# Two features of x are turned ahead of the first input projection, the other fourteen between the first projections, and the conditioning buffers are open from the start

## The chip, the cores and the metric

The kernel runs on one core of a Trainium2 chip. The metric is the device time of one execution in microseconds (us); lower is better. The engines are named as the profile names them: PE (matrix products and transposes; PEld is its weight load), DVE (vector), ACT (scalar, activations), POOL and SP. Nearly all loads are issued by SP.

## The reference

One step of a hybrid decoder: 256 prompt tokens and 8 x 8 sample tokens (320 in all), model width 2048. What matters here is its beginning:

```python
mod = silu(c) @ w_ada + b_ada                  # 9 conditioning rows, 6 * 2048 columns
sh1, sc1, gt1, sh2, sc2, gt2 = split(mod, 6)
h = rms_norm(x, g_pre_mix) * (1.0 + sc1) + sh1 # 320 tokens x 2048
proj = h @ w_in                                # qa, fa, ia, ga, qd, kvd, kpe_raw, gate_a, gate_b
...
# then: hgrn2 scan and latent attention over a paged cache, two output
# projections, gates, w_o, a second conditioned norm, and the 8192-wide MLP
```

## The kernel before

Every product is built in a way that keeps single precision: a weight tile is split into a rounded part `whi` (a cast on ACT, line 151) and a rest `wlo` (a subtraction on DVE, line 148); the activations are split likewise into `hh` and `hl`; three products are summed (lines 173 to 176). The activations lie feature-major: a "feature" here is a block of 128 of the 2048 columns, for all 320 tokens, so that there are sixteen.

**The start.** x is loaded token-major into three tiles `xt` (line 282). ACT and DVE take the mean square of each token and scale the tile (lines 442 to 448). Then the loop of lines 449 to 459 turns x into the feature-major tile `hraw`: for each of the sixteen features three transposes on PE (one for each `xt` tile) into a bank of the pool `aux` (four banks), and one copy from the bank into `hraw`, on DVE for even features (line 457) and on ACT for odd ones (line 455).

**Conditioning steps.** `ada_gen` (lines 318 to 333) computes `mod` a step at a time: one load of 1,024 KB of `w_ada` and 8 or 16 small products (`aux<-raw,cT` in the profile, x16 records for a step of the early form). The first eight steps make the scales and shifts of features 0 to 3, two steps for each of four pairs of features: steps 1 and 2 scale features 0 and 1, steps 3 and 4 shift them, steps 5 to 8 do the same for features 2 and 3. When a result is complete, it is turned by two transposes (`aux<-ident,adarow`) and added into `mod` (lines 306 to 316). Step 1 stands ahead of the loop over features; steps 2, 3 and 4 stand in it, after features 4, 10 and 15. Their loads go to the pool `wraw` (three buffers), which the weights of the projections use as well.

**First projections.** Behind the loop, `modulate(0, 2)` (lines 461 to 470) applies scale and shift to features 0 and 1 and splits them into `hh` and `hl`. Then come five chunks of features (line 532). In the first chunk (features 0 and 1) six calls of `partial` (lines 393 to 417) follow each other; each loads 512 KB of `w_in`, splits it and runs 24 products into four banks of the pool `acc`. Behind each of the first four of them stands one conditioning step (5 to 8), behind the second also `partial_kpe` (a 64 KB load and 6 products), and ahead of the sixth `modulate(2, 2)`. Steps 5 and later load into the pool `sraw` (three buffers), which line 531 opens only when the pool of the `xt` tiles has been closed: it takes their memory.

**Who sets the order.** The kernel is written as one stream. When it is built, a planner deals the instructions to the engines, each of which then runs its own queue strictly in that order; the planner keeps to the written order except where it reckons that an engine would stand idle and something further down could run. SP's queue of loads is such a queue too: a load whose buffer is not free holds those behind it.

**Memory.** Pools lie on two stacks, left and right; one that is opened where a closed one lay waits for the last readers there. `qst`, `lr` (`qn`, `kr`), `hraw` and the `xt` tiles lie on the left, in this order.

Of the kernel before, what the change touches and what calls it, by code (L numbers as in the profile page):

```python
# [7 lines left out]
F32 = mybir.dt.float32  # L8
# [3 lines left out]
AF = mybir.ActivationFunctionType  # L12
ALU = mybir.AluOpType
# [4 lines left out]
D = 2048  # L18
NP = 256
NB = 8  # L20
NT = 8
NS = NB * NT
N = NP + NS
P = 128
KF = D // P
# [56 lines left out]
def tile_hgrn2_mla_step(  # L82
# [9 lines left out]
    nc = tc.nc  # L92
# [10 lines left out]
    wraw = ctx.enter_context(tc.tile_pool(name="wraw", bufs=3))  # L103
# [37 lines left out]
    def mul(out, a, b, eng=None):  # L141
        (eng or nc.vector).tensor_tensor(out=out, in0=a, in1=b, op=ALU.mult)  # L142
# [75 lines left out]
    def rstd_of(x, tmp, r):  # L218

        nc.scalar.activation(out=tmp, in_=x, func=AF.Ln)  # L220
        last_exp[0] = nc.scalar.activation(out=r, in_=tmp, func=AF.Exp, scale=-0.5)
        mul(tmp, r, r)
        mul(tmp, tmp, x)
        nc.vector.tensor_scalar(out=tmp, in0=tmp, scalar1=-0.5, scalar2=1.5, op0=ALU.mult, op1=ALU.add)
        mul(r, r, tmp)

    def mean_eps(out, ps, n):
        nc.vector.tensor_scalar(out=out, in0=ps, scalar1=1.0 / n, scalar2=EPS, op0=ALU.mult, op1=ALU.add)
# [9 lines left out]
    def pool(name, bufs=1, side="left"):  # L238
        return tc.tile_pool(name=name, bufs=bufs, side=side, reuse_waits="tile")
# [13 lines left out]
    xsm = x_sample.rearrange("b t d -> (b t) d")  # L253
    TOK = ((0, 0, P), (1, P, P), (2, NP, NS))

    qst_stack = ExitStack()
    mq = qst_stack.enter_context(pool("mq"))
    qst = mq.tile([P, 6, NB, NS], F32, name="qst")
    lrstack = ExitStack()
    lr = lrstack.enter_context(pool("lr"))  # L260
    kvd = ckvT
    qn = lr.tile([P, RF, N], F32, name="qn")
    qd = qn
# [2 lines left out]
    xstack = ExitStack()  # L266
    xp = xstack.enter_context(pool("xp"))
    hraw = xp.tile([P, KF, N], F32, name="hraw")
    xqstack = ExitStack()
    xq = xqstack.enter_context(pool("xq"))  # L270
    xt = [xq.tile([P, D], F32, name=f"xt{i}") for i in range(3)]
# [27 lines left out]

    GA, GB = 5184, 7232  # L300
    SH1, SC1, GT1, SH2, SC2, GT2 = 0, 16, 32, 48, 64, 80
    araw = [wraw]

    turned = []

# [12 lines left out]
    def ada_gen():  # L318

        for b0, nb in [(SC1, 2), (SH1, 2), (SC1 + 2, 2), (SH1 + 2, 2)] + \  # L320
                [(m + f, 4) for f in (4, 8, 12) for m in (SC1, SH1)] + [(b0, 4) for b0 in range(GT1, 96, 4)]:
            ps = bank()
            nk = 16 // nb
            for r0 in range(0, KF, nk):
                raw, rv = load_w(w_ada, r0, nk, b0 * P, nb * P, araw[0])
                for k in range(nk):
                    mm(ps[32 * (k % 4):32 * (k % 4 + 1), 0:nb * P], cT[:, r0 + k], rv[:, k], r0 + k < 4, r0 + k >= KF - 4)
                if r0 == KF - nk:
                    row = adap.tile([P, 512], F32, name="adarow")
                    nc.scalar.copy(out=row[:, 0:nb * P], in_=ps[:, 0:nb * P])  # L330
                    turned.append((b0, nb, row))
                yield
                ada_turn()

    ada_steps = ada_gen()
# [57 lines left out]
    def partial(f0, nf, cols, outs):  # L393

        raw = wraw.tile([P, 2048], F32, name="raw")
        rv = raw[:, 0:nf * 512].rearrange("p (k c) -> p k c", c=512)
        rows = w_in[f0 * P:(f0 + nf) * P]
        if cols[1] == cols[0] + 256:
            nc.sync.dma_start(out=rv, in_=rows[:, cols[0]:cols[0] + 512].rearrange("(k p) c -> p k c", p=P))
        else:  # L400
            for i, c0 in enumerate(cols):
                nc.sync.dma_start(out=rv[:, :, 256 * i:256 * (i + 1)],
                                  in_=rows[:, c0:c0 + 256].rearrange("(k p) c -> p k c", p=P))
        ps = [bank(acc) for _ in range(4)]
        for k0 in range(0, nf, 2):
            hv, lv = split_w(rv, k0, 2, 512)
            for k in range(2):
                kk = f0 + k0 + k
                for m in range(4):
                    ms = slice(m * P, (m + 1) * P)  # L410
                    mm3(ps[m][:, 0:N], hv[:, k, ms], lv[:, k, ms], hh[:, kk], hl[:, kk],
                        k0 + k == 0, k0 + k == nf - 1)
        for m in range(4):
            if f0 == 0:
                nc.scalar.copy(out=outs[m], in_=ps[m][:, 0:N])
            else:
                add(outs[m], outs[m], ps[m][:, 0:N])
# [15 lines left out]
        else:  # L433
            add(kr, kr, ps[:, 0:N])

    with xqstack:
        junk = hraw.rearrange("p f n -> p (f n)")
        ssq = xq.tile([P, 3], F32, name="ssq")
        rr = xq.tile([P, 3], F32, name="rr")
        tt = xq.tile([P, 3], F32, name="tt")  # L440
        nc.vector.memset(ssq, 1.0)
        for i, t0, n in TOK:
            ss, rs = ssq[:, i:i + 1], rr[:, i:i + 1]
            nc.scalar.activation(out=junk[0:n, i * D // 2:i * D // 2 + D], in_=xt[i][0:n], func=AF.Square,
                                 accum_out=ss[0:n])
            mean_eps(ss, ss, D)
            rstd_of(ss, tt[:, i:i + 1], rs)
            nc.vector.tensor_scalar(out=xt[i][0:n], in0=xt[i][0:n], scalar1=rs[0:n], scalar2=None, op0=ALU.mult)
        for f in range(KF):
            ps = bank()  # L450
            fs = slice(f * P, (f + 1) * P)
            for i, t0, n in TOK:
                transpose(ps[:, t0:t0 + n], xt[i][0:n, fs], n)
            if f % 2:
                nc.scalar.copy(out=hraw[:, f], in_=ps[:, 0:N])
            else:
                nc.vector.tensor_copy(out=hraw[:, f], in_=ps[:, 0:N])
            if f in (4,10,15):
                next(ada_steps)

    def modulate(f0, nf):
        ada_turn()
# [63 lines left out]
        nc.scalar.dma_start(out=kpe_p[0, 0].rearrange("(i p) c -> p i c", p=P), in_=kt[:, 0:2])  # L526
        nc.scalar.dma_start(out=kpe_s[0].rearrange("b t c -> (b t) c"), in_=kt[0:NS, 2])

    p2stack, sstack, lstack, mstack = ExitStack(), ExitStack(), ExitStack(), ExitStack()
    partb = p2stack.enter_context(pool("p2", 1, "right")).tile([P, 4, 2, N], F32, name="partb")  # L530
    araw[0] = sstack.enter_context(pool("sraw", 3))
    chunks = ((0, 2, 4), (2, 2, 8), (4, 4, 8), (8, 4, 8), (12, 4, 0))
    modulate(0, 2)
    for q, (f0, nf, due) in enumerate(chunks):
        last = q == len(chunks) - 1
        for n, (cols, outs) in enumerate((
                ((4608, 4864), [kvd[:, f] for f in range(4)]),
                ((4096, 4352), [qd[:, f] for f in range(4)]),
                ((0, 1024), [part[:, i, j] for i in (0, 1) for j in range(2)]),
                ((2048, 3072), [part[:, i, j] for i in (2, 3) for j in range(2)]),  # L540
                ((GB, GB + 256), [partb[:, i, j] for i in (0, 1) for j in range(2)]),
                ((GA, GA + 256), [partb[:, i, j] for i in (2, 3) for j in range(2)]))):
            if n == 4 and last:
                araw[0] = wraw
                sstack.close()
                xstack.close()
                lr2 = lstack.enter_context(pool("lr2", 2, "right"))
                mp = mstack.enter_context(pool("mp"))
                lowrank_norms(lr2)
                qh = mp.tile([P, RF, N], F32R, name="qh")  # L550
                ql = mp.tile([P, RF, N], F32R, name="ql")
                split(qh, ql, qn)
                ch = mp.tile([P, RF, NP], F32R, name="ch")
                cl = mp.tile([P, RF, NP], F32R, name="cl")
                split(ch, cl, ckvT[:, :, 0:NP])

            if n == 5 and not last:
                turn_ = modulate(*chunks[q + 1][0:2])
            partial(f0, nf, cols, outs)
            for _ in range((0, (1, 1, 1, 1, 0, 0), (2, 2, 2, 1, 1, 0))[due // 4][n] if due else 0):  # L560
                next(ada_steps)
            if q == 3 and n == 0:
                nc.sync.dma_start(out=cst, in_=consts)
            if n == 1:
                partial_kpe(f0, nf)
                if q == 3:
                    with tc.issue_after(turn_.ins):
                        late_init()
# [6 lines left out]
    lstack.close()  # L575
    p2stack.close()
    init.close()


    nc.gpsimd.memset(qst[64:P, 4], 0.0)  # L580
# [8 lines left out]
    with mstack, pool("mp2", 2) as mp2:  # L589
# [126 lines left out]
        early_proj(0)  # L716
        for m in range(2):
            prompt_values(NH // 2 - 1, m, pend[0][m], pend[1])

    lrstack.close()  # L720


    ostack = ExitStack()
# [559 lines left out]
    with pool("zp") as zp, pool("zp2", 2) as zp2, pool("fraw", 3) as fraw:  # L1283
# [25 lines left out]
        for i, t0, n in TOK:  # L1309
            for j in range(2):  # L1310
# [4 lines left out]
                                     accum_out=ssq2[0:n, i, j:j + 1])  # L1315
# [18 lines left out]
        for q0 in range(0, KF, 2):  # L1334
# [3 lines left out]
            for j in range(2):  # L1338
                f = q0 + j
# [11 lines left out]
    with pool("ml1") as ml1, pool("ml2", 2) as ml2:  # L1351
# [4 lines left out]
        for c in range(NCH):  # L1356
# [19 lines left out]
            for g in range(8):  # L1376
                ps = gemm(w_down, 8 * c, 8, 256 * g, uh, ul)
                bk = out_banks() if last else None
                for m in range(2):
                    f = 2 * g + m  # L1380
# [11 lines left out]
        for q in range(4):  # L1392
            fs = slice(q * 512, (q + 1) * 512)
            for i, t0, n in TOK:
                nc.vector.scalar_tensor_tensor(  # L1395
                    out=zt[i][0:n, fs], in0=zt[i][0:n, fs], scalar=r[0:n, i:i + 1],
# [35 lines left out]
```

## Time and profile before

| | |
|---|---|
| median of 3 runs | 2153.34 us (2153.16 to 2161.1) |
| the profiled execution | 2156.85 us, of which its span is 2154.7 us |
| PE busy | 2105.6 us, 98% of the span |
| DVE / ACT / POOL busy | 1069.3 / 864.2 / 168.7 us |
| moved by DMA | 401.69 MB, mean 186 GB/s |

All times within the trace are counted from the start of the span. PE's busy time is modelled from a pipelined engine, so that a stretch of PE at 100% may still be one in which products follow each other at half the rate; the spacing of the starts tells that.

### The profile page before, as it was taken

The page shows a single profiled execution, that of the slowest core. Times are in us where ns is not written, and L with a number is a line of the kernel's source. Part 1 is how long each engine was busy: PE and PEld are TensorE (multiplying, and loading weights), DVE is VectorE, ACT ScalarE, POOL GpSimd, SP SyncE. Part 2 cuts the span into 40 slices and gives each one's busy share as a digit, 9 for nine tenths or more (in the row PEclk, how much of TensorE's full clock was granted, in tenths as well). Part 3 has the DMA queues.
Part 4 walks back from the last instruction along what each step waited for, and adds up shares of the span by engine and source line. Part 5 has one row for each costly group of instructions (what it writes and reads, how often), then busy time and mean ns, then how long its engine had stood idle before and what let it go on. Part 6 is the DMA issues. An engine that isn't in the chain of part 4 may idle for free.

```text
span 2154.7 us, 34719 instructions
## 1 busy us (share of the span) xinstructions
PE 2105.6 (98%) x14637; PEld 1906.8 (88%) x14637; DVE 1069.3 (50%) x1665; ACT 864.2 (40%) x1312; POOL 168.7 (8%) x167
## 2 busy tenths in 40 slices
PE   6999999999999999999999899999999999999997
PEld 3788989557788889999999599999999999999996
DVE  3555754445765646433544643444444444444455
ACT  4432453333545434333343543434343333333343
POOL 0000001103232211100010000000000000000001
PEclk9999999999999999999999899999999999999998
DMA  8986456444767768766854565445445445445442
GB/s 256 320 301 234 155 190 220 157 126 144 221 226 235 240 211 276 225 210 200 275 184 137 181 189 176 151 145 157 146 149 157 145 149 157 142 151 157 141 152 69
DMA packets 327571, 401.69 MB, mean 186 GB/s; under 512 B 10984, under 2 KB 265528, under 8 KB 324600
## 3 DMA queue, kind: packets, MB, share of 16 engines
q1 hardware_dynamic: 301576, 362.82, 52.3%
q0 software_dynamic: 3584, 21.50, 2.8%
q10 hardware_dynamic: 22256, 15.16, 2.3%
q8 instruction: 115, 1.88, 0.4%
q14 instruction: 40, 0.33, 0.0%
HBM read 387.44 MB, written 12.01 MB: 185 GB/s over the span
## 4 chain that ended last, share of the span: by engine, by line
PE 88%; issue 5%; DVE 3%; DMA 2%; ACT 1%; POOL 1%; SPq 0%; DVEq 0%; ACTq 0%; POOLq 0%
PE acc L136 76%; PE aux L136 8%; PE aux L139 4%; DMA raw<-in_w_in_dram 1%; DVE wlo L148 1%; POOL X L142 1%; ACT whi L151 1%; DMA raw<-in_w_ada_dram 1%; DMA xt<-in_x_prompt_dram 0%; DVE zu L1395 0%; DVE X L148 0%; DVE zg L142 0%; POOL qt L142 0%; ACT X L964 0%; DVE qn L499 0%
## 5 line engine op out<-in xcount | busy, mean ns | idle before, releaser
L148 DVE TENSOR_TENSOR wlo<-raw,whi 128x1024 fp32r<-128x1024 f32 (+1 forms) x493 | 603.8, 1230 | 706.2 <-ACT whi L151 703.5
L151 ACT CAST whi<-raw 128x1024 fp32r<-128x1024 f32 (+1 forms) x493 | 502.9, 1026 | 804.4 <-PE acc L136 665.9
L136 PE MATMUL acc<-hh,whi 128*128 128x320 f32 x1168 | 369.1, 317 | 3.5 <-ACT hh L151 2.3
L136 PE MATMUL acc<-hl,whi 128*128 128x320 f32 x1168 | 361.9, 310 | 0.3 <-DVE hl L148 0.3
L136 PE MATMUL acc<-hh,wlo 128*128 128x320 f32 x1168 | 360.7, 311 | 0.0
L136 PE MATMUL acc<-uh,whi 128*128 128x320 f32 x1024 | 316.7, 309 | 0.0
L136 PE MATMUL acc<-gh,whi 128*128 128x320 f32 x1024 | 316.7, 309 | 0.0
L136 PE MATMUL acc<-gh,wlo 128*128 128x320 f32 x1024 | 316.6, 309 | 0.0
L136 PE MATMUL acc<-gl,whi 128*128 128x320 f32 x1024 | 316.3, 309 | 0.0
L136 PE MATMUL acc<-uh,wlo 128*128 128x320 f32 x1024 | 316.1, 309 | 0.0
L136 PE MATMUL acc<-ul,whi 128*128 128x320 f32 x1024 | 316.1, 309 | 0.0
L136 PEld LDWEIGHTS acc<-hh,whi 128*128 128x128 f32 x1168 | 219.4, 188 | 34.6 <-issue 17.3
L136 PEld LDWEIGHTS acc<-hl,whi 128*128 128x128 f32 x1168 | 219.8, 188 | 2.9 <-DVE hl L148 1.4
L136 PEld LDWEIGHTS acc<-hh,wlo 128*128 128x128 f32 x1168 | 219.0, 188 | 3.0 <-DVE wlo L148 2.5
L136 PEld LDWEIGHTS acc<-gh,whi 128*128 128x128 f32 x1024 | 192.5, 188 | 1.9 <-ACT u L1365 0.8
L136 PEld LDWEIGHTS acc<-uh,whi 128*128 128x128 f32 x1024 | 192.6, 188 | 1.7 <-ACT u L1364 0.8
L136 PEld LDWEIGHTS acc<-gh,wlo 128*128 128x128 f32 x1024 | 192.6, 188 | 0.2
L136 PEld LDWEIGHTS acc<-gl,whi 128*128 128x128 f32 x1024 | 192.6, 188 | 0.0
L136 PEld LDWEIGHTS acc<-ul,whi 128*128 128x128 f32 x1024 | 192.4, 188 | 0.0
L136 PEld LDWEIGHTS acc<-uh,wlo 128*128 128x128 f32 x1024 | 192.4, 188 | 0.0
L136 PE MATMUL aux<-raw,cT 128*32 128x512 f32 (+1 forms) x832 | 115.2, 601 | 16.3 <-DVE tt L142 11.4
L145 POOL TENSOR_TENSOR ssum<-ssum,sqt 128x320 f32<-128x320 f32 x26 | 25.9, 997 | 981.2 <-ACT sqt L1245 980.3
(425 smaller groups left out, 2563.0 us busy)
## 6 DMA issues: line engine op xcount, KB each, us to landing
raw<-in_w_ada_dram SPq DMA_DIRECT2D x96, 1024.0 KB, 6.5
raw<-in_w_up_dram SPq DMA_DIRECT2D x64, 1024.0 KB, 5.7
raw<-in_w_down_dram SPq DMA_DIRECT2D x64, 1024.0 KB, 5.4
raw<-in_w_in_dram SPq DMA_DIRECT2D x60, 1024.0 KB, 5.4
raw<-in_w_o_dram SPq DMA_DIRECT2D x16, 1024.0 KB, 5.7
raw<-in_w_in_dram SPq DMA_DIRECT2D x20, 512.0 KB, 6.0
raw<-in_w_b_out_dram SPq DMA_DIRECT2D x8, 1024.0 KB, 5.8
raw<-in_w_a_out_dram SPq DMA_DIRECT2D x8, 1024.0 KB, 5.4
```

Of the source, the lines that this page charges most:

```text
L136: pe_last[0] = nc.tensor.matmul(out, lhsT=lhsT, rhs=rhs, start=start, stop=stop)
L139: pe_last[0] = nc.tensor.transpose(out=out, in_=in_, identity=ident[:k, :k])
L142: (eng or nc.vector).tensor_tensor(out=out, in0=a, in1=b, op=ALU.mult)
L145: (eng or nc.vector).tensor_tensor(out=out, in0=a, in1=b, op=ALU.add)
L148: return (eng or nc.vector).tensor_tensor(out=out, in0=a, in1=b, op=ALU.subtract)
L151: nc.scalar.copy(out=hi, in_=src)
```

## The change

The three tiles of x are scaled as before. Behind that, and ahead of the first projection, now stand: conditioning step 2, the turning of features 0 and 1 alone, conditioning steps 3 and 4. The other fourteen features are turned behind the first four calls of `partial`: 2, 4, 4 and 4 of them. The pool `sraw` is opened at the outset, below the pool of the `xt` tiles; steps 1, 2 and 4 load into it, step 3 into `wraw`. To make room, `lr` goes to the right stack, `qst` is opened only when `hraw` is closed, and `partb` (the results of the fifth and sixth call) only when the `xt` tiles are closed, ahead of the fifth call. `lr` is closed earlier, behind the five chunks.

```diff
@@
-    qst_stack = ExitStack()
-    mq = qst_stack.enter_context(pool("mq"))
-    qst = mq.tile([P, 6, NB, NS], F32, name="qst")
     lrstack = ExitStack()
-    lr = lrstack.enter_context(pool("lr"))
+    lr = lrstack.enter_context(pool("lr", 1, "right"))
...
     hraw = xp.tile([P, KF, N], F32, name="hraw")
+    sstack = ExitStack()
+    sraw = sstack.enter_context(pool("sraw", 3))
     xqstack = ExitStack()
...
-    araw = [wraw]
+    araw = [sraw]
...
+    def turn_x(f0, nf):
+        for f in range(f0, f0 + nf):
             ps = bank()
...
-            if f in (4,10,15):
-                next(ada_steps)
+
+    next(ada_steps)
+    turn_x(0, 2)
+    araw[0] = wraw
+    next(ada_steps)
+    araw[0] = sraw
+    next(ada_steps)
...
-    p2stack, sstack, lstack, mstack = ExitStack(), ExitStack(), ExitStack(), ExitStack()
-    partb = p2stack.enter_context(pool("p2", 1, "right")).tile([P, 4, 2, N], F32, name="partb")
-    araw[0] = sstack.enter_context(pool("sraw", 3))
+    p2stack, lstack, mstack = ExitStack(), ExitStack(), ExitStack()
+    partb = None
...
+            if q == 0 and n == 4:
+                xqstack.close()
+                partb = p2stack.enter_context(pool("p2", 1, "right")).tile([P, 4, 2, N], F32, name="partb")
...
                 lr2 = lstack.enter_context(pool("lr2", 2, "right"))
+                qst_stack = ExitStack()
+                qst = qst_stack.enter_context(pool("mq")).tile([P, 6, NB, NS], F32, name="qst")
...
             partial(f0, nf, cols, outs)
+            if q == 0 and n < 4:
+                turn_x((2, 4, 8, 12)[n], (2, 4, 4, 4)[n])
...
     init.close()
+    lrstack.close()
...
-    lrstack.close()
```

## Rows read from the trace of the kernel before

**Rows 1.** The page: the share of the chain that ended last by engine.

```profile
PE 88%; issue 5%; DVE 3%; DMA 2%; ACT 1%; POOL 1%; SPq 0%; DVEq 0%; ACTq 0%; POOLq 0%
```

**Rows 2.** Busy time by stretch: the stretch, its length, busy us (and instructions) of PE, PEld, DVE, ACT and POOL, then the granted clock of PE, the busy share of the DMA engines and GB/s.

```profile
17.00:20.00 3.00, 3.00 (x17) 1.52 (x10) 1.05 (x2) 0.46 (x3) 0.00 (x0) 1.00 1.10 347
...
15.60:34.20 18.60, 18.52 (x92) 8.65 (x92) 5.53 (x15) 3.25 (x9) 0.41 (x1) 1.00 0.62 187
...
41.00:44.40 3.40, 3.40 (x12) 2.26 (x12) 1.86 (x2) 0.00 (x0) 0.00 (x0) 0.51 1.11 340
44.40:73.70 29.30, 29.30 (x232) 26.20 (x231) 11.29 (x18) 18.04 (x36) 0.98 (x2) 1.00 0.89 301
73.70:112.00 38.30, 37.85 (x249) 27.13 (x248) 22.12 (x44) 10.81 (x12) 1.42 (x2) 1.00 0.98 343
```

**Rows 3.** The chain that ended last, in order of time, from 15 to 81 us: start, length, engine, tile and line.

```profile
36.48 1.03 PE aux L136 x14
...
38.00 0.45 PE aux L139 x2
...
40.72 1.29 PE acc L136 x4
42.02 0.99 PE aux L136 x2
...
46.76 0.99 PE aux L136 x14
...
73.96 1.04 PE aux L136 x8
...
75.02 6.23 DMA raw<-in_w_ada_dram
```

**Rows 4.** PE's matmuls and transposes in order of time: start, length of the group, tile out<-in, and in brackets the idle time before it.

```profile
15.68 1.94 PE L136 MATMUL aux<-raw,cT 128*32 128x256 f32 x16 [11.38 <-DVE tt L142]
17.55 0.28 PE L139 MATMUL aux<-ident,grow 16*128 16x16 f32 x1
...
17.98 4.58 PE L139 MATMUL aux<-ident,xt 128*128 128x128 f32 x15
22.49 1.93 PE L136 MATMUL aux<-raw,cT 128*32 128x256 f32 x16
24.36 5.55 PE L139 MATMUL aux<-ident,xt 128*128 128x128 f32 x18
...
43.38 0.47 PE L136 MATMUL acc<-hh,wlo 128*128 128x320 f32 x1
43.64 0.47 PE L136 MATMUL acc<-hl,whi 128*128 128x320 f32 x1
...
45.57 0.31 PE L136 MATMUL acc<-hh,wlo 128*128 128x320 f32 x1
45.72 0.31 PE L136 MATMUL acc<-hh,whi 128*128 128x320 f32 x1
```

**Rows 5.** The copies that follow the turning of features 12, 14 and 13 of x (DVE's timeline, then ACT's), for the rate of the transposes.

```profile
34.25 0.49 DVE L457 COPY hraw<-aux 128x320 f32<-128x320 f32 x1 [2.75 <-PE aux L139]
35.40 0.49 DVE L457 COPY hraw<-aux 128x320 f32<-128x320 f32 x1 [0.66 <-PE aux L139]
...
34.83 0.43 ACT L455 COPY hraw<-aux 128x320 f32<-128x320 f32 x1 [1.06 <-PE aux L139]
```

**Rows 6.** SP's queue from the start: issue time, length (with the waits inside a group), line and load.

```profile
4.83 13.20 SPq L161 DMA_DIRECT2D raw<-in_w_ada_dram  x4
24.48 8.33 SPq L399 DMA_DIRECT2D raw<-in_w_in_dram  x2
36.20 0.99 SPq L161 DMA_DIRECT2D raw<-in_w_ada_dram  x2
```

**Rows 7.** Transposes of the paged cache in a stage with the clock at its upper level (PE's timeline).

```profile
378.32 0.38 PE L139 MATMUL aux<-ident,craw 128*128 128x128 f32 x2
378.54 0.38 PE L139 MATMUL aux<-ident,raw 128*128 128x128 f32 x2
```

**Rows 8.** Busy time by stretch of the transposes alone (line 139): stretch, length, PE, PEld, granted clock, DMA share, GB/s.

```profile
376.00:446.00 70.00, 27.71 (x213) 22.58 (x212) 1.00 0.45 154
```

**Rows 9.** Who waited for whom from 38 to 74 us: total, times, longest.

```profile
DVE wlo L148 <- ACT whi L151: 15.7, 7, 5.3
```

**Rows 10.** POOL's timeline: the memsets of `qst`, and the first loads of the paged cache, which take memory of pools closed before.

```profile
0.75 0.52 POOL L580 MEMSET qst<- 64x512 f32 x1 [0.29 <-POOLq L1418]
...
254.10 1.90 POOL L142 TENSOR_TENSOR part<-part,lrsq 128x640 f32<-128x640 f32 x1 [46.08 <-ACT lrsq L473]
...
355.47 0.95 POOL L739 DMA_INDIRECT kraw<-in_cache_kpe_dram,pidx  x1 [0.30 <-issue]
356.73 0.93 POOL L748 DMA_INDIRECT craw<-in_cache_ckv_dram,pidx  x1 [0.30 <-issue]
```

**Rows 11.** PE's timeline where the stage of the paged cache begins.

```profile
365.23 0.84 PE L139 MATMUL aux<-ident,Sp 128*128 128x128 f32 x3
...
371.17 0.64 PE L139 MATMUL aux<-ident,craw 128*128 128x128 f32 x2
```

**Rows 12.** DMA issues of the stretch from 330 to 450 us: load, queue, count, median us from issue to landing.

```profile
craw<-in_cache_ckv_dram,pidx POOLq DMA_INDIRECT x10, 6.8
```

**Rows 13.** The first instructions that touch `qst` after the memsets (the tile's view: min/median/max ns, first and last start in us).

```profile
L664 ACT COPY qst<-qp x8: 239/244/245, 275.9 to 339.6; 64x64 f32<-64x64 f32 x8
```

More of the change, by code (lines that the diff above doesn't have):

```diff
@@ L434, in partial_kpe @@
             add(kr, kr, ps[:, 0:N])
[L436 to L449, printed above, removed]
+    junk = hraw.rearrange("p f n -> p (f n)")
+    ssq = xq.tile([P, 3], F32, name="ssq")
+    rr = xq.tile([P, 3], F32, name="rr")
+    tt = xq.tile([P, 3], F32, name="tt")
+    nc.vector.memset(ssq, 1.0)
+    for i, t0, n in TOK:
+        ss, rs = ssq[:, i:i + 1], rr[:, i:i + 1]
+        nc.scalar.activation(out=junk[0:n, i * D // 2:i * D // 2 + D], in_=xt[i][0:n], func=AF.Square,
+                             accum_out=ss[0:n])
+        mean_eps(ss, ss, D)
+        rstd_of(ss, tt[:, i:i + 1], rs)
+        nc.vector.tensor_scalar(out=xt[i][0:n], in0=xt[i][0:n], scalar1=rs[0:n], scalar2=None, op0=ALU.mult)
+    def turn_x(f0, nf):
+        for f in range(f0, f0 + nf):
             ps = bank()
@@ L540, in tile_hgrn2_mla_step @@
                 ((2048, 3072), [part[:, i, j] for i in (2, 3) for j in range(2)]),
-                ((GB, GB + 256), [partb[:, i, j] for i in (0, 1) for j in range(2)]),
-                ((GA, GA + 256), [partb[:, i, j] for i in (2, 3) for j in range(2)]))):
+                ((GB, GB + 256), (0, 1)), ((GA, GA + 256), (2, 3)))):
+            if q == 0 and n == 4:
+                xqstack.close()
+                partb = p2stack.enter_context(pool("p2", 1, "right")).tile([P, 4, 2, N], F32, name="partb")
+            if n >= 4:
+                outs = [partb[:, i, j] for i in outs for j in range(2)]
             if n == 4 and last:
```

## The prediction

> **What bounds the kernel now.** I read the page first: the chain that ended last lies on PE for 88% of the span [rows 1], so time is gained only where PE waits or runs at a lower rate than it could. Then the table of busy time by stretch, for the part that the change touches. PE is busy in nearly all of 15.6 to 34.2 us, but with slow work; from 44.4 to 73.7 us it is full, and from 73.7 to 112 us it lacks 0.45 us [rows 2]. Then the chain in order of time: step 4 of the conditioning ends at 37.51 us, the first product of the first projection starts at 40.72, and between the two PE does only the 0.45 us of turning the conditioning row [rows 3]. That is a wait of some 2.8 us with nothing to fill it, because every transpose of x stands ahead of it. Last, PE's own order of time, for its rate: six features are turned in 5.55 us from 24.36 on, 0.92 us each [rows 4], while features 12 to 14 follow each other at 0.57 us [rows 5]. The granted clock reads 1.00 in both places [rows 2], but the same shapes run slower in the first, so I go by durations there. [...]
>
> So the front loses time in two ways: fourteen features are turned at the slow rate ahead of the first projection, and PE waits ahead of it.
>
> **Part 1: what stands ahead of the first projection.** Before, step 1 runs at 15.68 us, and PE works without a break to 37.51 [rows 3, 4]. After, the order is step 1, two features, steps 2 to 4. Is the data there? Loads arrive at 347 GB/s [rows 2], so that a step's 1,024 KB take 3.0 us; step 1 had to wait for its load until 15.68 (the idle time in the row is put down to DVE work that does not feed it [rows 4]), so that steps 2, 3 and 4 can start at about 18.7, 21.7 and 24.7 us. A step takes 1.87 us (22.49 to 24.36), the small transposes behind step 1 0.43 us (17.55 to 17.98) [rows 4]. PE: step 1 and these to 17.98, step 2 to 20.6, two features of 0.92 us to 22.4, the first conditioning row (0.6 us at the slow rate, worked out from 0.45 [rows 3]) to 23.0, step 3 to 24.9, step 4 to 26.8. From the end of step 4 to the first product it took 3.21 us (37.51 to 40.72 [rows 3]); I add 0.2 us for the row at the slow rate. The first projection starts at 30.2 us instead of 40.72: 10.5 us earlier.
>
> Its weights must be there too. Their load was issued at 24.48 us, when step 2 had freed the buffer [rows 6]; now steps 1, 2 and 4 use other buffers, and it follows step 4's load directly: 512 KB more, there at about 26.2 us, with the cast and the subtraction inside the 3.4 us that PE waits for the conditioning anyway. Loads of steps 5 and 6 were held until 36.20, when the x tiles were free [rows 6]; now they wait for the products of steps 1 and 2. Nothing on SP is moved behind something later than before. I cost the loads at nothing; were the weights late, each us would count in full.
>
> **Part 2: the first projection.** From its start to the next piece it took 6.04 us (40.72 to 46.76, with 0.99 us of step 5 in a wait for `hl`) [rows 3]. Part of it ran at the lower clock level. After, PE comes to it with less work behind it; how long the lower level lasts there no row shows. Bounds: 24 products at 0.15 us and a wait of 0.9 make 4.5 us; at 0.26 us and with 0.99 they make 7.2 us [rows 3, 4]. I take 6.6, nearer to the slow end, as the stretch ahead of it is slow in the trace of before.
>
> **Part 3: the fourteen features.** 42 transposes on PE, seven copies on DVE and seven on ACT. The copies are cheap: ACT is busy 18.0 and DVE 11.3 of the 29.3 us to 73.7 [rows 2], and seven copies add 3.0 and 3.4 us (0.43 and 0.49 each [rows 5]). On PE they count. Some will fall into the wait of 3.4 - 0.6 = 2.8 us ahead of the first projection, since the planner fills idle time with later work: a memset of `qst`, written behind all five chunks, runs at 0.75 us [rows 10], and step 5 fills the wait for `hl` [rows 3]. Three features of 0.92 us fit. The other eleven cost 0.57 us each, the price of the same transposes at the higher rate [rows 5]: 6.3 us. Bounds: none fits and fourteen cost 8.0 us; five fit and nine cost 3 x 0.11 us each (two transposes of the cache start every 0.22 us [rows 7]), 3.0 us.
>
> **The sum.** Take the point at 73.96 us, where step 9 starts [rows 3]; the work from 46.76 to there, 27.2 us, is the same. After: 30.2 + 6.6 + 27.2 + 6.3 = 70.3, so 3.7 us are gained. The good ends: 30.2 + 4.5 + 27.2 + 3.0 = 64.9, 9.1 us. The bad ends: 30.2 + 7.2 + 27.2 + 8.0 = 72.6, 1.4 us.
>
> **Part 4: the memory moves.** `lr` on the other side, the earlier close of `lr` and the late `partb` cost nothing where their last readers are done: `partb` waits for the last transposes of x, which stand ahead of the fifth call anyway. The two memsets of `qst` (0.52 us each) move from 0.75 us to behind a product on POOL that ends at 256.0 [rows 10]; `qst` is first written at 275.9 [rows 13], so that 19.9 us hide 1.0 us; without that cover it would be 1.0 us. The pools behind `qst` slide down by the size of `lr`, so that the buffers for the paged cache lie on others of the attention's tiles; that is a rival below.
>
> **Behind 73.96 us** I carry the gain through: loads there are issued as buffers come free, which PE's own progress decides, so they move along.
>
> The profiled execution took 2156.85 us, its span 2154.7: 2153.1 us after, with a span of 2151.0. Against the median of 2153.34 us, 3.5 us lower, the forecast is **2149.6 us**, its own range 2144.2 to 2151.9.
>
> **The rivals.**
>
> *Copies that hold PE (the other side).* A moved transpose needs one of four `aux` banks, and a bank comes free only by its copy, which now stands in DVE's and ACT's queues amid the splitting of weights. DVE waited seven times for ACT's cast, 15.7 us in all [rows 9], 2.2 us each; a copy queued behind such a wait holds PE. One such wait in each of the four groups costs 9.0 us: 2153.3 - 3.7 + 9.0 = 2158.6. It outweighs the gain from 0.9 us a group on. For it: the groups of four fill all banks, which conditioning steps share. Against it: both engines are idle much of the time [rows 2], and a copy takes less than its feature. Chance 0.10.
>
> *Turning costs the clock.* In 15.6 to 34.2 us PE, busy all along, with much turning, stayed slow [rows 2, 4]. If each group of transposes between projections brought the lower level for as long as from 41.0 to 44.4 us [rows 2], it would cost 3.4 x 0.49 = 1.7 us, four groups 6.8: 2156.4 us. It decides from the third group on. Against it: from 376 to 446 us transposes are 27.7 of 70 us, and the clock is 1.00 throughout [rows 8]. [...] Chance 0.06.
>
> *The loads take it back.* From 73.7 to 112 us the DMA engines are busy 0.98 of the time, and a piece of 6.23 us on a conditioning load lies on the chain [rows 2, 3]. If that stretch is set by the loads and not by PE, it ends where it did: 2153.3 us. Against it: PE lacks only 0.45 us there [rows 2]. Chance 0.09.
>
> *A later load of the cache.* The first `craw` load is issued at 356.73 us [rows 10]; 6.8 us later it is there [rows 12], for transposes at 371.17 [rows 11]. If the new places make POOL's queue wait until the transposes of `Sp` end at 366.07 [rows 11], it lands at 372.9, 1.7 us late: 2151.3 us. Chance 0.08.
>
> *The order is not what is written.* If the planner puts the transposes ahead of the first projection all the same, PE has the same 21.8 us from 15.68 to 37.51 and then the row's 0.45, without the wait: 37.96 instead of 40.72, a gain of 2.8 us [rows 3, 4], 2150.5. Chance 0.07.
>
> **How the numbers follow.** Forecast 0.60, rivals 0.10, 0.06, 0.09, 0.08, 0.07. The range 2144.0 to 2156.5 us holds all but the first rival and some hundredths of other mishaps. What a measurement of this kernel can tell from no change is about 0.5%, 10.8 us. Even the good ends stop at 9.1 us, so faster by more has 0.03; the dearest rival loses 5.3 us, so slower by more has 0.03; 0.94 lie between.
>
> **What would show it.** In the changed profile the first `acc<-hh,whi` should start near 30 us, steps 2 to 4 near 18.7, 21 to 23 and 25 us, and three or so features be turned ahead of it. From there to the step behind the next chunk PE should show no idle time before transposes (a wait on `hraw` copies is the first rival), and the granted clock should stay at 1.00 once it is up (else the second). The step at 73.96 should come near 70 us, and the same gap should still stand at 112, 260 and 376 us; where it shrinks, the rival of that place was right. I am wrong in the main if the first projection starts early and the point at 73.96 does not move.

## The result: some 4.5 us slower, and the profile after

| | before | after |
|---|---|---|
| median of 20 runs | 2153.8 us (2151.35 to 2161.16) | 2158.92 us (2154.47 to 2165.14) |
| ratio after / before | | 1.0021, interval 1.0011 to 1.003 |
| the profiled execution | 2156.85 us | 2155.09 us, span 2153.3 us |

The changed kernel takes 4.5 us more (0.0021 x 2153.8; interval 2.4 to 6.5). Here and below a ratio and its interval are worked out from all runs of both kernels; it is not the ratio of the two medians, which lie 5.1 us apart here. The change is less than 0.5%, to which I had given 0.94, but it has the other sign than my forecast of 2149.6 us, and the median lies 2.4 us above the upper end of my range, 2156.5. The profiled execution of after happens to be one of its shortest; the last section says why its total must not be used alone.

**The front did what it should.** PE's order of time, in the same columns as [rows 4]:

```profile
15.80 1.93 PE L136 MATMUL aux<-raw,cT 128*32 128x256 f32 x16 [11.50 <-DVE tt L142]
...
18.09 1.33 PE L139 MATMUL aux<-ident,xt 128*128 128x128 f32 x4
19.36 1.94 PE L136 MATMUL aux<-raw,cT 128*32 128x256 f32 x16
...
22.21 1.07 PE L136 MATMUL aux<-raw,cT 128*32 128x256 f32 x16
24.74 1.07 PE L136 MATMUL aux<-raw,cT 128*32 128x256 f32 x16 [1.47 <-DMA raw<-in_w_ada_dram]
26.35 0.44 PE L139 MATMUL aux<-ident,adarow 128*128 128x128 f32 x2 [0.54 <-ACT adarow L329]
26.62 1.16 PE L139 MATMUL aux<-ident,xt 128*128 128x128 f32 x6
29.27 0.85 PE L136 MATMUL acc<-hh,whi 128*128 128x320 f32 x4 [1.49 <-ACT hh L151]
...
46.21 2.30 PE L139 MATMUL aux<-ident,xt 128*128 128x128 f32 x12
```

The four steps stand at 15.80, 19.36, 22.21 and 24.74 us; two features (six transposes at 26.62) fit into the wait ahead of the first projection; this starts at 29.27 instead of 40.72. Four features at 46.21 take 2.23 us to the next instruction at 48.44, 0.56 us each.

**The chain** in order of time, the columns of [rows 3], around the point that answers to 73.96:

```profile
68.54 1.04 PE aux L136 x8
...
69.60 7.59 DMA raw<-in_w_ada_dram
...
77.23 1.07 PE aux L136 x8
```

The point has come 5.4 us forward, from 73.96 to 68.54. Then PE waits 2.13 us for a conditioning load, by its own row:

```profile
77.23 1.07 PE L136 MATMUL aux<-raw,cT 128*32 128x512 f32 x8 [2.13 <-DMA raw<-in_w_ada_dram]
```

From 73.7 to 108.5 us PE is idle for 2.26 us in after and for 0.45 in before, so that 1.9 of the 5.4 us are given back. From 108 to 360 us the same instructions of PE stand 3.56 us earlier than before.

**Then the gain is lost in one place**, where the paged cache begins. POOL's order of time (before: [rows 10], where the same two loads are issued at 355.47 and 356.73 with no wait), then PE's, both of after:

```profile
366.97 0.95 POOL L750 DMA_INDIRECT kraw<-in_cache_kpe_dram,pidx  x1 [15.37 <-PE aux L136]
368.23 0.94 POOL L759 DMA_INDIRECT craw<-in_cache_ckv_dram,pidx  x1 [0.31 <-issue]
```

```profile
365.05 1.65 PE L136 MATMUL aux<-PTp,vv 128*128 128x128 f32 x6
374.08 0.66 PE L139 MATMUL aux<-ident,craw 128*128 128x128 f32 x2 [7.38 <-DMA craw<-in_cache_ckv_dram,pidx]
...
380.60 1.02 PE L136 MATMUL acc<-wlo,qst 128*64 128x512 f32 x4
```

POOL stands 15.37 us at the load of `kraw`, whose buffer is released by a product of PE (`aux` at line 136). The load of `craw` is behind it in the same queue. PE finishes the products `aux<-PTp,vv` and stands idle for 7.38 us. The chain says the same, step by step:

```profile
365.12 1.59 PE aux L136 x6
366.71 0.26 issue
366.97 0.95 POOL kraw L750
367.93 0.31 issue
368.23 5.71 DMA craw<-in_cache_ckv_dram,pidx
373.94 0.14 issue
374.08 5.35 PE aux L139 x24
```

0.26 + 0.95 + 0.31 + 5.71 + 0.14 = 7.37 us: the whole wait. In before the same six products and the `craw` transposes behind them follow each other without a gap:

```profile
369.73 1.65 PE L136 MATMUL aux<-PTp,vv 128*128 128x128 f32 x6
371.17 0.64 PE L139 MATMUL aux<-ident,craw 128*128 128x128 f32 x2
...
376.87 1.03 PE L136 MATMUL acc<-wlo,qst 128*64 128x512 f32 x4
```

So PE is 4.68 us ahead at the `vv` products (365.05 against 369.73), 2.91 us behind at the first `craw` (374.08 against 371.17), and 3.72 us behind from the products of `wlo` on (380.60 against 376.87), a loss of 3.56 + 3.72 = 7.3 us in the stage. The granted clock (the column behind POOL's) in the windows of after, then of before, has a part in what the wait of 7.38 us does not explain:

```profile
364.00:368.00 4.00, 2.70 (x17) 2.38 (x16) 1.02 (x4) 0.00 (x0) 0.95 (x1) 0.50 0.00 0
368.00:372.00 4.00, 0.00 (x0) 0.00 (x0) 0.00 (x0) 0.00 (x0) 2.85 (x4) 0.50 0.81 240
372.00:376.00 4.00, 1.92 (x9) 1.95 (x10) 0.00 (x0) 0.59 (x1) 1.86 (x2) 0.50 1.01 422
376.00:380.00 4.00, 4.00 (x19) 3.33 (x19) 1.91 (x3) 1.17 (x2) 0.00 (x0) 0.50 1.00 422
```

```profile
368.00:372.00 4.00, 4.00 (x27) 3.98 (x27) 1.02 (x4) 0.00 (x0) 0.00 (x0) 0.50 0.68 272
372.00:376.00 4.00, 4.00 (x24) 3.83 (x22) 1.38 (x2) 1.54 (x3) 0.00 (x0) 0.57 0.12 39
376.00:380.00 4.00, 4.00 (x25) 2.08 (x26) 1.99 (x3) 0.80 (x2) 0.37 (x1) 1.00 0.00 0
```

Both kernels fall to the lower level (0.50) here, among products of 8 columns (`128x8`) and small transposes; in after, the wait falls into it and it lasts to 380 us instead of 375.4. From the first `craw` to the products of `wlo` after takes 6.52 us (374.08 to 380.60) and before 5.70 (371.17 to 376.87): the 0.8 us between 2.91 and 3.72. On the other side, after reaches the lower level later in the order of its work: the three transposes of `Sp` ahead of the `vv` products take 0.84 us in before [rows 11] and 0.49 in after, and by the `vv` products the 3.56 us have grown to 4.68. The two nearly cancel, so that the loss of 7.3 us is about the wait itself.

### The profile page after: what moved, and what is told of

It is laid out like the page before. It is cut to its first block, busy times and chain, and to the rows that moved or that the text cites. A ratio compares the mean times of both kernels' runs of the same rounds, so it can differ in the third digit from the quotient of the medians.

```text
span 2153.3 us, 34711 instructions
## 1 busy us (share of the span) xinstructions
PE 2095.7 (97%) x14637; PEld 1902.3 (88%) x14637; DVE 1073.2 (50%) x1665; ACT 863.2 (40%) x1312; POOL 167.2 (8%) x167
## 4 chain that ended last, share of the span: by engine, by line
PE 87%; issue 4%; DVE 3%; DMA 3%; ACT 1%; SPq 1%; POOL 1%; DVEq 0%; ACTq 0%; POOLq 0%
PE acc L136 76%; PE aux L136 8%; PE aux L139 4%; DMA raw<-in_w_ada_dram 1%; DVE wlo L148 1%; DMA raw<-in_w_in_dram 1%; ACT whi L151 1%; SPq L161 0%; DVE zu L1406 0%; DVE X L148 0%; DMA craw<-in_cache_ckv_dram,pidx 0%; POOL qt L142 0%; DVE zg L142 0%; DVE bb L956 0%; POOL X L142 0%
```

## The experiments

**My theory.** `lr` (`qn` and `kr`, 4 x 320 and 320 values, 6,400 bytes of each partition) has left the left stack, so the attention's pools lie 6,400 bytes lower. The first `kraw` buffer now covers a tile `vv` that the last products `aux<-PTp,vv` read, and in POOL's queue the small load, which waited 15.37 us in after, held the large ones behind it. The front itself gains what I forecast.

**The rivals.** Against this theory stand three others: the time is lost because POOL and the load work arrive differently behind an earlier PE, not because of the layout; or the clock alone costs it; and, for the front, that the open conditioning buffers give the gain and not the order of the turning.

### The order of the loads (two kernels)

After, with the `craw` loads of the first two sequences issued ahead of `kraw`:

```diff
             kraw = sc.tile([P, 8, 64], F32, name="kraw")
-            nc.gpsimd.indirect_dma_start(out=kraw.rearrange("p j c -> p (j c)"), out_offset=None, in_=kpe_rows,
-                                         in_offset=off)
+
+            def load_kraw():
+                nc.gpsimd.indirect_dma_start(out=kraw.rearrange("p j c -> p (j c)"), out_offset=None, in_=kpe_rows,
+                                             in_offset=off)
+
+            if b >= 2:
+                load_kraw()
             craws = []
...
+            if b < 2:
+                load_kraw()
             return kraw, craws
```

> The changed kernel, with one difference: for the first two sequences of the paged cache the two large loads (craw) are issued ahead of the small one (kraw); PE's order is the same as in the changed kernel. Theory (queue): the two small loads now lie on memory that the attention's last products (vv) read until 366.6 us, and hold the craw loads behind them in POOL's queue; with craw ahead, its first load is issued near 352 us, PE does not wait 7.4 us at 366.7, and the 3.6 us gained ahead of it are kept: 2150.2 us, 0.998 of before. The small load itself still waits to about 367 us and is needed only some 7 us after the stage's start, so that it costs at most 1 us. Rival (clock): the loss is the longer stretch at the lower clock level (17.1 us in the changed kernel, 10.2 us before); then the order of the loads changes little and the time stays at 2157 to 2159 us.

Measured: 2152.29 us against 2153.56, ratio 0.9985 (0.9971 to 0.9999). POOL, then PE, of this run:

```profile
350.85 0.94 POOL L764 DMA_INDIRECT craw<-in_cache_ckv_dram,pidx  x1 [0.30 <-issue]
367.36 0.95 POOL L752 DMA_INDIRECT kraw<-in_cache_kpe_dram,pidx  x1 [15.57 <-PE aux L136]
```

```profile
365.44 1.65 PE L136 MATMUL aux<-PTp,vv 128*128 128x128 f32 x6
366.88 0.64 PE L139 MATMUL aux<-ident,craw 128*128 128x128 f32 x2
```

`kraw` waits as long as in after, 15.57 us, and it harms nothing: the first `craw` is issued 16.5 us ahead of it and PE has no gap. PE stands 4.62 us ahead of the kernel before at 360 us and again from 376 us on (4.29 in the rows shown, which lie within the lower clock level). The memory conflict is still there; what cost the time was its place at the head of the queue. Between after and this kernel lie 0.0036, 7.8 us (some 4 to 11 us by the two intervals), against the 7.3 us read from the trace.

The same exchange in the kernel before:

> The kernel before with the order of the cache's loads of x1_swap, nothing of the change. Theory (queue): before, neither small load waits, so that putting the large ones ahead gives nothing: the first transposes of the cache stay at 371 us, 2153.6 us, 1.000 of before. Rival: the order of x1_swap is better by itself, whatever the places; then this kernel gains what x1_swap gained over x2_hole, 1 to 2 us. It is a second trace of the front of before as well.

Measured: 2154.09 against 2153.5 us, ratio 0.9997 (0.998 to 1.0013). Where no `kraw` waits, the exchange is worth nothing that shows.

### The layout alone, and the layout put back

Before, with nothing but `lr` moved to the right stack and closed where after closes it; the front is unchanged:

```diff
-    lr = lrstack.enter_context(pool("lr"))
+    lr = lrstack.enter_context(pool("lr", 1, "right"))
...
     init.close()
+    lrstack.close()
...
-    lrstack.close()
```

> The kernel before, with lr on the right stack and closed ahead of the attention, and nothing else of the change; PE's order is that of before. Theory (queue): this alone brings the wait: the first kraw load near 370 us in place of 355.5, PE idle for about 7 us ahead of the first transposes of the cache, 7.3 us slower than before: 2161 us, 1.0034. Rival: the loss comes of the new order of the front, by way of the clock or of the loads of 69 to 113 us; then this kernel takes 2153.8 us as before.

Measured: 2167.63 against 2153.56 us, ratio 1.0054 (1.0034 to 1.0074), from five runs: 11.6 us, more than after itself loses. POOL, then PE:

```profile
371.17 0.95 POOL L738 DMA_INDIRECT kraw<-in_cache_kpe_dram,pidx  x1 [17.01 <-PE aux L136]
```

```profile
369.24 1.65 PE L136 MATMUL aux<-PTp,vv 128*128 128x128 f32 x6
378.40 0.66 PE L139 MATMUL aux<-ident,craw 128*128 128x128 f32 x2 [7.51 <-DMA craw<-in_cache_ckv_dram,pidx]
```

The same wait, 7.51 us, without any change of the front. PE goes from 1.0 us ahead of before to 7.9 us behind, a loss of 8.9 us. So the layout alone does it; after's 4.5 us are net of what the front gains, and here the front gains nothing by the edit. The 1.4 us beyond the wait fall into a longer stretch at the lower clock level, 20.5 us against 10.2 in before (worked out from the granted clock in windows of 4 us; it is 0.50 from 364 to 384 us here). The 8.9 us lie within the interval of the measured loss, 7.3 to 15.9 us; why its middle is higher stays open with five runs.

After, with an unused tile of 6,400 bytes (and a memset of one column of it) that puts the later attention pool back to its old place:

```diff
+    hole = mstack.enter_context(pool("hole")).tile([P, 1600], F32, name="hole")
+    nc.gpsimd.memset(hole[:, 0:1], 0.0)
     with mstack, pool("mp2", 2) as mp2:
```

> The changed kernel, with an unused tile of 6,400 bytes a partition (the size of qn and kr together) between the pools mp and mp2, so that the attention's tiles lie under the buffers of the paged cache as they did before; one memset of a column on POOL is added. Theory (queue): no small load waits, the first craw load is issued near 353 us (before: 356.7, less 3.6), PE does not wait, 2150.2 us, 0.998 of before. Rival (clock): as the changed kernel, 2157 to 2159 us. If x1_swap is fast and this one is not, it is the queue's order but not the place of lr that matters.

Measured: 2153.8 against 2153.56 us, ratio 0.9994 (0.9978 to 1.001). POOL, then PE:

```profile
353.75 0.95 POOL L752 DMA_INDIRECT kraw<-in_cache_kpe_dram,pidx  x1 [0.31 <-issue]
```

```profile
369.44 1.65 PE L136 MATMUL aux<-PTp,vv 128*128 128x128 f32 x6
370.88 0.63 PE L139 MATMUL aux<-ident,craw 128*128 128x128 f32 x2
```

`kraw` is issued at 353.75 and `craw` at 355.01 without a wait, and PE goes from the `vv` products to `craw` without a gap. The wait is gone: PE is 1.71 us ahead of before at 360 us and still 0.94 us ahead from 376 us on. But the front gained only 1.8 us in this trace, because its first projection ran at the lower clock level (0.54 from 28.5 to 36 us, below), and the total, forecast at 0.998, shows no gain.

Two smaller tiles, one run each. With 512 values (2,048 bytes, one `kraw` buffer or one `vv` tile):

> The kernel of x2_hole with the unused tile cut to 2,048 bytes a partition. Worked out from the sizes of the tiles: the buffer of the first small load still lies on the second vv tile, which the last products read. Theory (the place of vv): the first kraw load waits until these products end, and PE is idle for about 7 us ahead of the first transposes of the cache, as in the changed kernel. Rival (any shift loosens it): no wait.

2158.33 us: `kraw` waits 14.96 us, PE 7.43 us for `craw`; 3.82 us ahead become 1.90 behind.

```profile
366.30 0.95 POOL L752 DMA_INDIRECT kraw<-in_cache_kpe_dram,pidx  x1 [14.96 <-PE aux L136]
```

```profile
373.46 0.66 PE L139 MATMUL aux<-ident,craw 128*128 128x128 f32 x2 [7.43 <-DMA craw<-in_cache_ckv_dram,pidx]
```

With 768 values:

> The same with 3,072 bytes: now the first small load's buffer lies on the first vv tile, read for the last time some 20 us earlier, and the second one's on the second vv tile. Theory (the place of vv): the first kraw load and the first craw load go at about 353 us, the second kraw load waits to about 366 us with the craw loads behind it, which are needed only at 380; PE does not wait ahead of the first transposes. Rival (lr's full size is needed): the wait stays about 7 us.

2152.8 us. POOL:

```profile
351.53 0.95 POOL L752 DMA_INDIRECT kraw<-in_cache_kpe_dram,pidx  x1 [0.30 <-issue]
352.79 0.94 POOL L761 DMA_INDIRECT craw<-in_cache_ckv_dram,pidx  x1 [0.30 <-issue]
367.64 0.95 POOL L752 DMA_INDIRECT kraw<-in_cache_kpe_dram,pidx  x1 [13.91 <-PE aux L136]
```

Now the first `kraw` is free and the second waits 13.91 us. Its followers come late, but PE has the first `craw` (transposed at 367.16 without a wait) to work on, and no time is lost: 3.95 us ahead on both sides. 1,024 bytes decide between a loss of 5.7 us and none. Which tile lies under which buffer I take from the releaser in these rows and from the sizes, not from addresses. These two are single runs, and their totals would prove little; the rows of the waits carry the argument.

### The two halves of the front

Both with the tile of 6,400 bytes, so that the cache stage is not in the way. First the early conditioning buffers alone: all sixteen features are turned ahead of the first projection, the steps in their old places.

```diff
+    turn_x(0, 5)
     next(ada_steps)
-    turn_x(0, 2)
+    turn_x(5, 6)
     araw[0] = wraw
     next(ada_steps)
     araw[0] = sraw
+    turn_x(11, 5)
     next(ada_steps)
...
-            if q == 0 and n < 4:
-                turn_x((2, 4, 8, 12)[n], (2, 4, 4, 4)[n])
```

> The kernel of x2_hole with all sixteen features turned ahead of the first projection, steps 2 to 4 behind features 4, 10 and 15 as in the kernel before: the early buffers without the moved turning. Theory (the moved turning gives the gain): the first projection starts near 40 us, the wait ahead of it stays, and the point at which step 9 starts stays within 1 us of 73.96: 2153 us, 1.000 of before. Rival (the early loads give it): that point comes near 69 us and the time is that of x2_hole.

Measured: 2153.78 against 2153.56 us, ratio 0.9995 (0.9981 to 1.001). In the trace the first product stands at 43.55, behind a wait of 2.28 us, and step 9 at 77.69 instead of 73.96; PE stays 3.25 us behind from 100 to 340 us. That is later than either theory said, which had 73 to 75 and 69 us: the front stayed at its slow rate longer (products 0.27 us apart until 48.8 us). In this trace the open buffers alone bring nothing forward.

Then the turning alone: `sraw` is opened only ahead of the fifth call, and steps 1 to 8 load through `wraw`.

```diff
-    sraw = sstack.enter_context(pool("sraw", 3))
...
-    araw = [sraw]
+    araw = [wraw]
...
                 xqstack.close()
+                araw[0] = sstack.enter_context(pool("sraw", 3))
```

> The kernel of x2_hole with the turning moved, but the pool of the conditioning buffers opened only when the x tiles are closed, ahead of the fifth call of the first chunk; until then steps 1 to 8 load into the three buffers of the weights: the moved turning without the early buffers. Theory (both parts are needed): the loads of steps 4 to 8 and of the first projections wait for each other's buffers, PE waits for them in 25 to 70 us, and step 9 starts at 74 us or later: 2154 to 2160 us. Rival (the turning alone gives the gain): step 9 starts near 70 us and the time is that of x2_hole.

Measured: 2152.55 against 2153.5 us, ratio 0.9992 (0.9975 to 1.0009). The first product comes at 30.68 us, so the early start is the order of the turning. Step 9 begins at 67.98, but only two of its products; the other fourteen come at 72.67. At 100 us PE is 0.73 us behind before: the early start is spent. SP shows one cause, the loads of the steps:

```profile
62.16 11.99 SPq L161 DMA_DIRECT2D raw<-in_w_ada_dram  x2
```

Two issues take 11.99 us with the wait for a buffer, and those behind them move too. The forecast time, 2154 to 2160 us, was missed: 2152.55 us is not clear of before either way. So in its one trace neither half alone has PE ahead of before at 100 us. That each half needs the other is not shown by this: neither ratio differs from 1 by more than its interval, and both fronts were longer at the slow rate than after's (with the turning alone the granted clock is 0.57 from 28.5 to 36 us). The share that each half has of the 3.7 us stays open.

## Why the prediction was wrong, point by point

- **What stands ahead of the first projection: right in time, in part by luck.** Steps at 15.80, 19.36, 22.21, 24.74 us (forecast: step 1, then 18.7, 21 to 23, 25). First product 29.27, forecast 30.2. But the sum let PE's own work set these times, with 1.87 us a step. Steps 3 and 4 took 1.07 us each, and step 4 waited 1.47 us for its load, which arrived near the 24.7 us that I had worked out for it.
- **The first projection: its good bound.** It took 4.55 us (29.27 to 33.82, where the next step begins on the chain), forecast 6.6, bound 4.5: in this run the upper clock level was there from the first product on (1.00 from 29.2 to 33.9 us). In the run with the tile of 6,400 bytes it was not (0.54 from 28.5 to 36 us), and there the front gained 1.8 us instead of 3.6.
- **The fourteen features: right.** 0.56 us each (forecast 0.57); two fitted ahead, not three. The rival "turning costs the clock" falls here: the 12 transposes at 46.21 us take 2.23 us, the products behind them (from 49.81 us) start 0.15 us apart, and the granted clock is 1.00 from 44.4 to 68.5 us. Between the projections this trace shows no harm from turning.
- **The point of step 9: 68.54, forecast 70.3** (own bounds 64.9 to 72.6). 5.4 us gained, then 1.9 us given back, most of it in the wait of 2.13 us for a load: the rival "the loads take it back" holds for a part. In the run with exchanged loads, whose front is the same program, no such wait came: 4.8 us ahead at this point, 5.26 at 140 us.
- **The gain of the front: right in size.** Ahead of the cache stage (at 140 us) the five traces with this front stand 3.56, 5.26, 1.79, 3.92 and 3.94 us ahead of before; their mean is 3.7, the forecast 3.7. Two more traces of the old front (before with exchanged loads, and with `lr` alone moved) stand 0.03 and 1.00 us ahead of before; against the mean of all three old fronts the gain is 3.4 us. In after itself the match of 3.56 with 3.7 is in part luck: the first projection took 2.05 us less than I had taken, and the loads behind 73.96, put at nothing, took back 1.9.
- **Copies that hold PE: fell.** PE's rows show no wait on a copy of `hraw` in the front, and its weight loads wait 0.8 us in all.
- **The step that failed is in Part 4: the pools that slide down by the size of `lr`.** The sum has them at nothing and leaves them to the rival "a later load of the cache", taken at 1.7 us and 0.08, where the stage lost 7.3 us. The memsets of `qst`, the other cost weighed there, ran at 207 us in POOL's idle time. I had the place and the mechanism, a load of POOL's queue that waits for memory of the attention, and mis-sized it in two ways. I let the wait end with the transposes of `Sp` at 366.07, with 5.1 us of PE's work still between them and the `craw` transposes at 371.17 to cover most of the 6.8 us of the load. The waiting buffer is released by the `vv` products, the last work ahead of those transposes, so nothing covers it: the full 5.71 us of the load count. And I left out POOL's own time for the load that is first in the queue (0.95 us and two short steps). By the rows that I had, 1.26 us of `kraw` (355.47 to 356.73 in [rows 10]) and 6.8 us of landing [rows 12] make 8.1 us; the trace says 7.4. As both the release and the need come from PE's own order, the wait did not depend on how early PE arrives: 7.38 us in after, 7.51 us with the front of before.
- **And the chance was wrong.** Which tile lies under a moved buffer can be worked out from the sizes of the pools, without a chip. I said that the buffers "lie on others of the attention's tiles" and gave that 0.08 instead of finding out which.

The sum: 3.56 us of gain less 7.3 us of loss is 3.7 us slower in the matched rows; measured 4.5 (2.4 to 6.5). The range ended at 2156.5, because the only rival I let in above it was the copies.

**What may beat both.** The changed kernel with the loads of `craw` ahead of `kraw`: 0.9985 (0.9971 to 0.9999), 3.2 us below before. The upper end of its interval is just under 1, and the kernel with the tile of 6,400 bytes, which has the same front and no wait either, is at 0.9994 (0.9978 to 1.001). So the front's gain is shown in the traces, and in the totals by one kernel of two.

## What to carry to other kernels

When a change moves or frees a buffer, list what now lies under each buffer behind it, down to the tile, and ask for each load whose product releases it and how much of the consumer's work stands between that release and the first use; a front that gains 3.7 us is easily paid for with one load that waits, some 300 us later. In an in-order queue put the load that somebody waits for first and the one whose memory comes free late behind it: here that exchange of loads was worth 7.8 us in one kernel and nothing where the memory was free. And follow the gain through the trace at the same instructions, stage by stage; the totals of the two profiled executions would have said that the change helps.

## What the hardware showed that I had not expected

**The wait for memory stood on POOL, the issuing engine, with all that was behind it.** Six indirect loads, issued without a wait from 353.75 to 360.94 us with the tile of 6,400 bytes, left POOL from 366.97 to 374.17 us in after, because the first of them waited 15.37 us. The wait stands in POOL's row, and the DMA share in after is 0.00 from 364 to 368 us, in before 1.01.

**The same instructions got different clock levels.** With the same order in the front, the first projection ran at 1.00 in after and, but for its end, at the lower level with the tile of 6,400 bytes (0.54 from 28.5 to 36 us), where the same four products take 1.44 us instead of 0.85:

```profile
29.64 1.44 PE L136 MATMUL acc<-hh,whi 128*128 128x320 f32 x4 [1.50 <-ACT hh L151]
```

At 1,200 us, far from the change, the lower level lasted about 10 us in the profiled execution of after and about 20 us in that of before. Windows of after, then of before:

```profile
1203.00:1207.00 4.00, 2.52 (x14) 0.59 (x11) 2.10 (x10) 2.63 (x7) 0.00 (x0) 0.50 1.05 388
1207.00:1211.00 4.00, 4.00 (x20) 1.40 (x18) 3.49 (x15) 0.79 (x2) 0.00 (x0) 0.69 1.05 389
1211.00:1215.00 4.00, 4.00 (x24) 2.05 (x24) 3.74 (x13) 3.57 (x7) 0.89 (x2) 1.00 0.80 285
```

```profile
1207.00:1211.00 4.00, 4.00 (x17) 2.00 (x20) 2.27 (x9) 2.75 (x6) 0.88 (x2) 0.50 0.89 322
1211.00:1215.00 4.00, 4.00 (x16) 1.56 (x9) 2.49 (x8) 2.38 (x4) 0.45 (x1) 0.50 0.01 5
1215.00:1219.00 4.00, 4.00 (x20) 2.55 (x19) 1.32 (x6) 1.26 (x3) 0.45 (x1) 0.56 0.00 0
```

Around there after goes from 3.6 us behind before to 1.4 us ahead, 5.0 us that belong to no edit: the run of before with exchanged loads, the same program there, gains 4.4 us on before from the products of `wlo` in the cache stage to the end of the span. By these two points, six of the traces gain 4.4 to 5.4 us on before (after; the tile of 6,400 bytes; `lr` alone; the two halves of the front; before with exchanged loads), and the other three (after with exchanged loads; the two smaller tiles) lie within 0.1 us. This accounts for most of the 6.9 us by which the profiled executions (after 1.8 us shorter) and the medians (after 5.1 us longer) disagree. Why the length differs, no run here shows.
